# Attention's two ends in a decoder block: filler pieces placed earlier at the start, the first mixing row placed earlier at the end

## The chip, the cores and the metric

The kernel runs on one core of a Trainium2 chip. A core has a matrix engine (TensorE, PE in the profile, whose weight loads are listed apart as PEld), a vector engine (VectorE, DVE), a scalar engine (ScalarE, ACT), GpSimd (POOL), and SyncE (SP), which here only issues DMA transfers. SBUF is the on-chip memory for operands, and PSUM holds the results of matmuls in eight banks. The metric is the device time of one execution in microseconds; the time of a kernel is the median over its runs.

## The reference

One block of a decoder: 2048 tokens of width 1024. A combined projection gives queries, keys, values (8 heads of 64 channels) and 512 pooling channels `u`. Half of the mixed output is stick-breaking attention, half a pooled mean of `u`; both go through one output projection, and a SwiGLU network of width 2816 follows.

```python
h = rmsnorm(x, g_mix_pre[l]) * (1.0 + scale_m) + shift_m
q, k, v, u = jnp.split(h @ w_in[l], [SB_WIDTH, 2 * SB_WIDTH, 3 * SB_WIDTH], axis=-1)
...
# stick_breaking_attention, for each block of 128 queries
z = jnp.einsum('bhqd,bhkd->bhqk', qb, kb) * inv_sqrt
mask = s_idx < t_idx
log1m = jnp.where(mask, -jax.nn.softplus(z), 0.0)
after = lax.cumsum(log1m, axis=3, reverse=True) - log1m
w = jnp.where(mask, jnp.exp(jax.nn.log_sigmoid(z) + after), 0.0)
out = jnp.einsum('bhqk,bhkd->bhqd', w, vb)
...
mix = jnp.concatenate([attn, pool], axis=-1) @ w_out[l]
x = x + gate_m * rmsnorm(mix, g_mix_post[l])
h = rmsnorm(x, g_ffn_pre[l]) * (1.0 + scale_f) + shift_f
f = (jax.nn.silu(h @ w_gate[l]) * (h @ w_up[l])) @ w_down[l]
x = x + gate_f * rmsnorm(f, g_ffn_post[l])
```

A weight is the sigmoid of its own score times the product of the sigmoids of the negated scores between key and query. The kernel computes that product as a running product over the keys, from the last to the first.

## The kernel before

The program goes through a prologue (conditioning, the first half of the projections), attention (about 273 to 789 us), the mixing rows and the feed-forward network. Products that must be exact in float32 are made of three matmuls each: an operand is split into a rounded part and the rest (`split`, L56 to L60: a cast on ScalarE at L59, a subtract on VectorE at L60), and `mm3` (L63 to L71) adds high by high, high by low and low by high.

**Attention.** A unit is a head, a block of 512 queries and a block of 512 keys, `(h, tb, sc)`. There are 80 units, first all heads for the query blocks 0 and 1, then all heads for 2 and 3. A unit has four steps of 128 queries each, so there are 320 steps, and `n` counts them. What a step does runs through the engines:

- `weights_step` makes the scores `z` on TensorE (L926, L927), and two sigmoids on ScalarE, `sg` of the score (L929) and `pr` of the negated score (L931). It puts the block into the list `scans`.
- `scan_step` makes the running product on VectorE (L942 on a diagonal unit, L945 elsewhere; the order lists name this instruction SCALAR_TENSOR_TENSOR, the trace TENSOR_TENSOR_SCAN), with small copies of the carry on GpSimd (L941, L944, L948), and multiplies by `sg` on GpSimd into `w` (L950).
- `turn_step`, seven steps later (`OFF`), transposes four tiles of `w` on TensorE (L961) into `wt` and splits that: cast `wth` on ScalarE, subtract `wtl` on VectorE.
- `values_step`, two steps behind (`LAG`), adds the products with the values into `av` (L976, L977). The last one of a query block copies `av` to `o` (L981), and two DMAs of SyncE's queue store it to DRAM as a high and a low part, `mtd` and `mld` (L983).

PSUM banks in attention: the scores take `z0` and `z1` in turn, the transposes `w0`, `w1` and `a1`, the values `a0`, the filler pieces `mm`. Bank `z2` holds `begin`, a constant of the scans.

**Fillers.** The projections of the second half of the tokens are cut into pieces and put between the steps. A piece is three matmuls (L69 to L71) of 128x512; eight pieces make a tile of q, k or u, and the last one is followed at once by its evacuation, for q and k a cast (L59) and a subtract (L60), then a DMA store (L362). A ninth turn of each tile is empty. The loop takes as many pieces by step `n` as `goal` says: `START // 2` before attention, one more a step up to `START`, then in proportion to the attention work done.

**Loads.** `block_loads` allocates a query tile `qt` from two buffers and loads it by two DMAs (L876), keys by two more (L882) and values by one (L883). A query tile can be loaded only when the last score of the tile two back is done. Names in the lists are `qt4_1` for head 4, query block 1, and `o1_3_0` for the output of head 3, query block 0; `kd0_3` is the stored key tile of heads 0 and 1 for tokens 1536 to 2047.

**Mixing rows.** A row of 128 tokens is loaded (`mix_load`: attention's high and low part and the pooled half, L1036 and L1044), summed on GpSimd (`mix_add`, L1048), split into `mh` and `ml` in two halves of four 128-channel tiles (`mix_split`), and multiplied with the output weights in 16 pieces (`mix_products`, a bank of `f_ps` for each half of the columns). Rows 0 and 4 come first in the sequence, and `FIRST_LOADS`, `FIRST_ADDS` and `FIRST_SPLITS` say at which `n` they are loaded, added and split.

**What sets the order.** On TensorE, ScalarE, VectorE and GpSimd the instructions stand in the order in which the code writes them (`manual_schedule`, L147): the loop below is the schedule. The order of the DMAs on SyncE's queue is not written by hand; the framework's scheduler sets it when the kernel is built, and the queue issues them in that order, each waiting for its own condition. So an edit in the loop can also change the order of DMAs that the edit does not name.

## Time and profile before

| what | value |
|---|---|
| time of the runs, median of 3 | 2256.32 us (2255.94 to 2257.32) |
| the profiled execution's own time | 2255.57 us |
| its span, first to last instruction | 2253.8 us |
| TensorE busy | 2229.1 us, 99% |
| VectorE busy | 1624.3 us, 72% |
| GpSimd busy | 1267.2 us, 56% |
| ScalarE busy | 1167.7 us, 52% |
| mean granted TensorE clock | 0.999 |

Times in the profile count from the span's start. A row of the timeline gives the start, the busy time, the engine, the line, the operation, output and inputs by the program's names without their numbers, the shapes and a count; in brackets stands how long the engine sat idle before it and whose work ended that. Matmuls are pipelined: a busy time of 0.39 us belongs to one that starts 0.23 us after the one before. The shares of busy time are averages over the whole program, and attention has other ones than the feed-forward network.

### The profile page before, as it was taken

Reading aid. Unit: us, or ns where it says so; the run is one execution under the profiler, and the core shown is the slowest. Engines: PE = TensorE matmul, PEld = TensorE weight load, DVE = VectorE, ACT = ScalarE, POOL = GpSimd, SP = SyncE. Lnnn points to the kernel's source line nnn. Section 1 sums busy time; section 2 is a strip of 40 time slices with the busy share of each in tenths; the row PEclk is TensorE's granted clock in tenths of the full one; section 3 lists DMA queues with packets and bytes.
Section 4 is the critical chain, followed back from the end, with each engine's and each line's share of the span. In section 5 each row is a group of like instructions: output and inputs, shape, how many; then the busy total and the mean of one; then the engine's idle time right before and its main releaser. Section 6 shows DMA issues by size and latency. Waiting matters only on the chain.

```text
span 2253.8 us, 33256 instructions
## 1 busy us (share of the span) xinstructions
PE 2229.1 (99%) x10613; PEld 1844.2 (82%) x10613; DVE 1624.3 (72%) x2227; ACT 1167.7 (52%) x2425; POOL 1267.2 (56%) x1579
## 2 busy tenths in 40 slices
PE   8999999999999999999999999999999999999998
PEld 6888888888888888878888888888888888888887
DVE  7874599999999957666565656787866565655566
ACT  6335599898999944453232323555532323234444
POOL 1452277787779955546868687221677565651003
PEclk9999999999999999999999999999999999999999
DMA  9996877534443556665454556777853333328664
GB/s 318 341 285 214 282 196 190 147 105 119 121 118 104 175 173 219 216 198 178 157 166 154 165 163 205 262 226 244 254 168 122 94 117 94 112 91 296 216 188 149
DMA packets 323980, 413.55 MB, mean 183 GB/s; under 512 B 20630, under 2 KB 189146, under 8 KB 323676
## 3 DMA queue, kind: packets, MB, share of 16 engines
q1 hardware_dynamic: 319196, 408.81, 57.0%
q10 hardware_dynamic: 4608, 2.63, 0.4%
q8 instruction: 83, 1.36, 0.2%
q14 instruction: 93, 0.76, 0.1%
HBM read 282.90 MB, written 128.45 MB: 183 GB/s over the span
## 4 chain that ended last, share of the span: by engine, by line
PE 88%; DVE 5%; ACT 2%; issue 2%; DMA 2%; POOL 1%; SPq 0%; DVEq 0%; ACTq 0%; POOLq 0%
PE wt L961 4%; PE t_u L70 3%; PE t_u L69 3%; PE t_u L71 3%; PE t_g L69 3%; PE t_g L70 3%; PE t_g L71 3%; PE dn1p L69 3%; PE dn1p L70 3%; PE dn1p L71 3%; PE b_u L69 3%; PE dn0p L71 3%; PE b_u L70 3%; PE b_u L71 3%; PE dn0p L70 3%; PE dn0p L69 3%
## 5 line engine op out<-in xcount | busy, mean ns | idle before, releaser
L950 POOL TENSOR_TENSOR w<-sg,pr 128x512 f32<-128x512 f32 (+2 forms) x320 | 306.6, 958 | 46.8 <-DVE pr L945 16.1
L1335 POOL TENSOR_TENSOR s<-s,cu 128x512 f32<-128x512 f32 x88 | 131.8, 1504 | 237.3 <-DVE cu L1334 141.8
L945 DVE TENSOR_TENSOR_SCAN pr<-pr,carry,begin 128x512 f32<-128x512 f32 x192 | 243.8, 1270 | 0.0
L929 ACT ACTIVATE sg<-z 128x512 f32<-128x512 f32 (+2 forms) x320 | 184.1, 575 | 50.9 <-PE z L927 40.8
L60 DVE TENSOR_TENSOR wtl<-wt,wth 128x512 fp32r<-128x512 f32 (+1 forms) x320 | 189.1, 591 | 18.1 <-ACT wth L59 16.1
L59 ACT CAST wth<-wt 128x512 fp32r<-128x512 f32 (+1 forms) x320 | 183.4, 575 | 12.1 <-PE wt L961 12.1
L931 ACT ACTIVATE pr<-z 128x512 f32<-128x512 f32 (+2 forms) x320 | 183.6, 574 | 0.0
L961 PE MATMUL wt<-ident,w 128*128 128x128 f32 x1088 | 172.6, 273 | 1.9 <-POOL pr L941 1.1
L60 DVE TENSOR_TENSOR u_s_l<-u_s,u_s_h 128x512 fp32r<-128x512 f32 x66 | 64.2, 972 | 150.0 <-ACT u_s_h L59 150.0
L961 PEld LDWEIGHTS wt<-ident,w 128*128 128x128 f32 x1088 | 134.1, 140 | 33.3 <-POOL pr L941 1.8
L1325 ACT ACTIVATE s<-s 128x512 f32<-128x512 f32 x88 | 55.7, 633 | 184.1 <-DVE s L1324 184.1
L976 PE MATMUL av<-wth,vt 128*128 128x512 f32 (+1 forms) x320 | 126.4, 395 | 0.9 <-ACT o L981 0.8
L60 DVE TENSOR_TENSOR u_a_l<-u,u_a_h 128x512 fp32r<-128x512 f32 x66 | 75.6, 1147 | 64.1 <-ACT u_a_h L59 64.1
L977 PE MATMUL av<-wtl,vt 128*128 128x512 f32 (+1 forms) x320 | 118.1, 369 | 1.9 <-DVE wtl L60 1.6
L69 PE MATMUL dn0p<-w0p_h,g0p_h 128*128 128x512 f32 x308 | 119.8, 389 | 0.0
L70 PE MATMUL dn0p<-w0p_l,g0p_h 128*128 128x512 f32 x308 | 119.8, 389 | 0.0
L71 PE MATMUL dn0p<-w0p_h,g0p_l 128*128 128x512 f32 x308 | 119.8, 389 | 0.0
L926 PE MATMUL z<-kt,qt 128*128 128x512 f32 (+2 forms) x320 | 118.6, 371 | 0.7 <-ACT pr L931 0.6
L59 ACT CAST g_s_h<-g_s 128x512 fp32r<-128x512 f32 x66 | 39.5, 621 | 152.1 <-POOL g_s L1267 76.0
L927 PE MATMUL z<-kt,qt 128*128 128x512 f32 (+2 forms) x320 | 116.9, 365 | 0.0
L59 ACT CAST u_s_h<-u_s 128x512 fp32r<-128x512 f32 x66 | 38.6, 614 | 150.8 <-POOL u_s L1267 149.0
L69 PE MATMUL dn1p<-w1p_h,g1p_h 128*128 128x512 f32 x292 | 113.6, 389 | 0.0
(655 smaller groups left out, 7178.4 us busy)
## 6 DMA issues: line engine op xcount, KB each, us to landing
g<-in_w_gate_dram SPq DMA_DIRECT2D x42, 512.0 KB, 5.4
u<-in_w_up_dram SPq DMA_DIRECT2D x42, 512.0 KB, 4.1
wc<-in_w_cond_dram SPq DMA_DIRECT2D x32, 512.0 KB, 7.5
qt<-qd SPq DMA_DIRECT2D x64, 256.0 KB, 4.0
kt<-kd SPq DMA_DIRECT2D x96, 128.0 KB, 3.2
vt<-vd SPq DMA_DIRECT2D x48, 256.0 KB, 4.1
wd<-in_w_down_dram SPq DMA_DIRECT2D x44, 256.0 KB, 3.3
tdt<-wd SPq DMA_DIRECT2D x44, 256.0 KB, 2.0
```

The costliest lines, as they stand in the source:

```text
L59: nc.scalar.copy(hi, src)
L60: low.tensor_tensor(lo, src, raw(hi), ALU.subtract)
L69: nc.tensor.matmul(ps, lh, rh, start=first and i == 0, stop=False)
L70: nc.tensor.matmul(ps, lh, rl, start=False, stop=False)
L71: nc.tensor.matmul(ps, ll, rh, start=False, stop=last and i == n - 1)
L929: nc.scalar.activation(sg[:, 0:L], z[:, 0:L], AF.Sigmoid, scale=0.125)
L931: nc.scalar.activation(pr[:, 0:L], z[:, 0:L], AF.Sigmoid, scale=-0.125)
L945: nc.vector.tensor_tensor_scan(keys, keys, begin, carry, ALU.mult, ALU.bypass)
L950: nc.gpsimd.tensor_tensor(w[:, 0:L], sg[:, 0:L], pr[:, 1:L + 1], ALU.mult)
L961: nc.tensor.transpose(wt[:, i * P:(i + 1) * P], wss[u][i][:, b * P:(b + 1) * P], ident)
L976: nc.tensor.matmul(av[:, lo0:], vb, wh[:, lo0:], start=first, stop=False)
L1335: nc.gpsimd.tensor_tensor(s, s, u, ALU.mult)
```

## The change

The start: `START` goes from 6 to 8, so four pieces instead of three stand before attention and eight instead of six are taken by its fourth step. A clause runs a scan at once at `n < 4`, where the loop otherwise keeps one back.

The end: row 0 is loaded 18 steps before the end of the scores instead of 14, added 11 instead of 6, and split 6 instead of 3. `EARLY_PIECES` (four, since `HK` is 4) of its products are put one by one behind the last four steps with scores, and the bank for them is `mm`, which the fillers have left by then; the cycle of the later banks starts one place further.

```diff
-    START = 6
+    START = 8
...
-    f_ps = bank_cycle("z0", "z1", "z2", "mm", "w0", "w1", "a0", "a1")
+    f_ps = bank_cycle("mm", "z0", "z1", "z2", "w0", "w1", "a0", "a1")
...
-    FIRST_LOADS = (len(steps) - 14, len(steps) - 10)
-    FIRST_SPLITS = (len(steps) - 3, len(steps) + 2)
-    FIRST_ADDS = (len(steps) - 6, len(steps) - 1)
-    PER_STEP = 3
+    FIRST_LOADS = (len(steps) - 18, len(steps) - 10)
+    FIRST_SPLITS = (len(steps) - 6, len(steps) + 2)
+    FIRST_ADDS = (len(steps) - 11, len(steps) - 1)
+    PER_STEP, EARLY_PIECES = 3, HK
...
-        if len(scans) > 1 or n >= len(steps) and scans:
+        if len(scans) > 1 or (n < 4 or n >= len(steps)) and scans:
             scan_step(*scans.pop(0))
...
         if n >= len(steps):
             mix_pieces(PER_STEP)
+        elif n >= len(steps) - EARLY_PIECES and products:
+            mix_pieces(1)
```

Three places show what this moves. A row gives the line, the operation, the output and the inputs with the numbers of the program's names, and the shape.

ScalarE at attention's start, before: the sigmoids of the first unit's blocks, `sg0_0_0_i` and `pr0_0_0_i`, and the cast of the finished q tile `q0_2`.

```order
L931 ACTIVATE pr0_0_0_1_2677<-z0_0_0_1_2672 128x256
L929 ACTIVATE sg0_0_0_2_2689<-z0_0_0_2_2686 128x384
L931 ACTIVATE pr0_0_0_2_2691<-z0_0_0_2_2686 128x384
L929 ACTIVATE sg0_0_0_3_2706<-z0_0_0_3_2703 128x512
L931 ACTIVATE pr0_0_0_3_2708<-z0_0_0_3_2703 128x512
L59 CAST q0_2_2717<-q0_2_2649 128x512
L929 ACTIVATE sg0_1_1_0_2732<-z0_1_1_0_2729 128x128
```

The same place after:

```order
L931 ACTIVATE pr0_0_0_1_2684<-z0_0_0_1_2679 128x256
L929 ACTIVATE sg0_0_0_2_2696<-z0_0_0_2_2693 128x384
L931 ACTIVATE pr0_0_0_2_2698<-z0_0_0_2_2693 128x384
L59 CAST q0_2_2710<-q0_2_2649 128x512
L929 ACTIVATE sg0_0_0_3_2717<-z0_0_0_3_2714 128x512
L931 ACTIVATE pr0_0_0_3_2719<-z0_0_0_3_2714 128x512
L929 ACTIVATE sg0_1_1_0_2736<-z0_1_1_0_2733 128x128
```

The cast of the q tile moved from behind the fourth block's sigmoids to ahead of them. VectorE has the same order there in both kernels: scan of `pr0_0_0_2`, evacuation of `q0_2`, scan of `pr0_0_0_3`.

SyncE's queue in the middle of the first half, before: the query tile of head 4, block 1, in two halves, a key store, the output of head 3, block 0, and the next query tile.

```order
L983 DMA mtd1_97<-o1_2_1_3759 64x512
L983 DMA mld1_101<-o1_2_1_3759 64x512
L876 DMA qt4_1_3939<-qd2_1_69 64x2x512 x2
L362 DMA kd0_3_79<-k0_3_3834 128x2x512
L983 DMA mtd0_96<-o1_3_0_3869 64x512
L983 DMA mld0_100<-o1_3_0_3869 64x512
L876 DMA qt5_0_4145<-qd2_0_68 64x2x512 x2
```

The same place after (`wu0_1_32` is a chunk of projection weights):

```order
L983 DMA mtd1_97<-o1_2_1_3767 64x512
L983 DMA mld1_101<-o1_2_1_3767 64x512
L446 DMA wu0_1_32_5060<-in_w_in_dram 128x8x128
L362 DMA kd0_3_79<-k0_3_3792 128x2x512
L876 DMA qt4_1_3945<-qd2_1_69 64x2x512
L983 DMA mtd0_96<-o1_3_0_3873 64x512
L983 DMA mld0_100<-o1_3_0_3873 64x512
L876 DMA qt4_1_3945<-qd2_1_69 64x2x512
L876 DMA qt5_0_4155<-qd2_0_68 64x2x512 x2
```

A weight load and the key store moved ahead of the query tile, and its second half moved behind the two stores of head 3's output. In the same way one of a pair of key loads moved ahead of head 2's query tile.

VectorE at attention's end, before: the scans (`pr`), the subtracts behind the transposes (`wtl`), and the low part of mixing row 0 (`ml_0`).

```order
L60 TENSOR_TENSOR wtl7_3_3_3_11070<-wt7_3_3_3_11067,wth7_3_3_3_11069 128x128
L945 SCALAR_TENSOR_TENSOR pr7_3_1_2_11059<-pr7_3_1_2_11059,carry7_3_2_2_10981,begin_2659 128x512
L60 TENSOR_TENSOR wtl7_3_2_0_11102<-wt7_3_2_0_11096,wth7_3_2_0_11101 128x512
L945 SCALAR_TENSOR_TENSOR pr7_3_1_3_11088<-pr7_3_1_3_11088,carry7_3_2_3_11005,begin_2659 128x512
L60 TENSOR_TENSOR wtl7_3_2_1_11128<-wt7_3_2_1_11122,wth7_3_2_1_11127 128x512
L945 SCALAR_TENSOR_TENSOR pr7_3_0_0_11114<-pr7_3_0_0_11114,carry7_3_1_0_11043,begin_2659 128x512
L60 TENSOR_TENSOR wtl7_3_2_2_11152<-wt7_3_2_2_11146,wth7_3_2_2_11151 128x512
L60 TENSOR_TENSOR ml_0_11158<-m32_0_10858,mh_0_11157 128x512 x2
L945 SCALAR_TENSOR_TENSOR pr7_3_0_1_11140<-pr7_3_0_1_11140,carry7_3_1_1_11063,begin_2659 128x512
```

The same place after:

```order
L60 TENSOR_TENSOR wtl7_3_3_3_11071<-wt7_3_3_3_11068,wth7_3_3_3_11070 128x128
L60 TENSOR_TENSOR ml_0_11082<-m32_0_10748,mh_0_11081 128x512 x2
L945 SCALAR_TENSOR_TENSOR pr7_3_1_2_11060<-pr7_3_1_2_11060,carry7_3_2_2_10982,begin_2662 128x512
L60 TENSOR_TENSOR wtl7_3_2_0_11108<-wt7_3_2_0_11102,wth7_3_2_0_11107 128x512
L945 SCALAR_TENSOR_TENSOR pr7_3_1_3_11094<-pr7_3_1_3_11094,carry7_3_2_3_11006,begin_2662 128x512
L60 TENSOR_TENSOR wtl7_3_2_1_11134<-wt7_3_2_1_11128,wth7_3_2_1_11133 128x512
L945 SCALAR_TENSOR_TENSOR pr7_3_0_0_11120<-pr7_3_0_0_11120,carry7_3_1_0_11044,begin_2662 128x512
L60 TENSOR_TENSOR wtl7_3_2_2_11162<-wt7_3_2_2_11156,wth7_3_2_2_11161 128x512
```

The pair `ml_0` moved ahead of three scans. On TensorE the row's first four pieces stand, one each, behind the transposes `wt7_3_2_1`, `wt7_3_2_2`, `wt7_3_2_3` and `wt7_3_1_0`. From the feed-forward network on, TensorE's order is the same in both.

## The prediction

> **What bounds the kernel now.** I read the page's first part and its chain that ended last, then a table of busy time by stage, then single rows at the three places where the change moves work.
>
> ```profile
> span 2253.8 us, 33256 instructions
> PE 2229.1 (99%) x10613; PEld 1844.2 (82%) x10613; DVE 1624.3 (72%) x2227; ACT 1167.7 (52%) x2425; POOL 1267.2 (56%) x1579
> PE 88%; DVE 5%; ACT 2%; issue 2%; DMA 2%; POOL 1%; SPq 0%; DVEq 0%; ACTq 0%; POOLq 0%
> ```
>
> TensorE is busy for 2229.1 of 2253.8 us, and the change leaves every matmul in place. So only TensorE's waits can shrink or grow: 24.7 us in the whole program. The next table has, for four stretches of attention, TensorE, its weight loads, VectorE, ScalarE and GpSimd as busy us with a count, then the granted clock, DMA share and GB/s.
>
> ```profile
> 275.00:285.00 10.00, 8.67 (x44) 6.78 (x43) 7.20 (x9) 8.15 (x21) 5.63 (x17) 1.00 1.06 271
> 285.00:345.00 60.00, 59.26 (x349) 49.94 (x348) 58.71 (x84) 55.08 (x140) 45.31 (x102) 1.00 0.70 186
> 500.00:700.00 200.00, 200.00 (x1132) 168.33 (x1131) 197.55 (x248) 181.72 (x401) 161.05 (x349) 1.00 0.43 120
> 780.00:795.00 15.00, 13.99 (x72) 10.66 (x73) 14.43 (x18) 11.71 (x25) 12.98 (x24) 1.00 0.79 288
> ```
>
> At the start TensorE is idle 1.33 of 10 us, at the end 1.01 of 15; between them it is nearly full, with VectorE at 58.71 of 60 us (98%) beside it. The overlapped ends of matmuls hide some idle time in these sums, so below I measure a wait as a row's start less the end that the rows before imply at the usual spacing of 0.23 us for a 128x512 matmul. Both ends together hold about 4.3 us of waits (1.8, 1.8 and 0.7, below), which is 0.19%: the change cannot be worth more unless it mends something elsewhere. I count a difference within 0.2%, 4.5 us, as none that a measurement of this kernel can tell.
>
> **Start: two more pieces ahead of the first transpose.**
>
> ```profile
> 276.23 0.40 PE L69 MATMUL q<-hth,wq_h 128*128 128x512 f32 x1
> 276.92 0.40 PE L926 MATMUL z<-kt,qt 128*128 128x512 f32 x1
> 278.72 0.38 PE L926 MATMUL z<-kt,qt 128*128 128x256 f32 x1 [0.31 <-ACT pr L931]
> 279.55 0.45 PE L926 MATMUL z<-kt,qt 128*128 128x384 f32 x1 [0.33 <-ACT pr L931]
> 282.37 0.33 PE L961 MATMUL wt<-ident,w 128*128 128x128 f32 x1 [0.69 <-POOL pr L941]
> ```
>
> One filler piece is three matmuls: 276.92 - 276.23 = 0.69 us. The three bracketed waits, taken from the spacing, cost 0.47, 0.49 and 0.85 us: 1.8 together. Now the engines that they wait for.
>
> ```profile
> 278.55 0.59 ACT L59 CAST q<-q 128x512 fp32r<-128x512 f32 x1
> 279.17 0.69 DVE L60 TENSOR_TENSOR q<-q,q 128x512 fp32r<-128x512 f32 x1 [1.51 <-ACT q L59]
> 279.78 3.19 DVE L942 TENSOR_TENSOR_SCAN pr<-pr,zero,begin 128x512 f32<-128x512 f32 x4
> 281.22 1.09 POOL L950 TENSOR_TENSOR w<-sg,pr 128x512 f32<-128x512 f32 x1 [2.52 <-ACT pr L931]
> ```
>
> The fourth transpose waits for the multiply at 281.22, which waits for the scan at 279.78, which stands behind the evacuation of the finished q tile at 279.17. With START at 8 the q tile's last piece runs one step earlier, its cast ahead of the fourth score's sigmoids, and VectorE evacuates it while those still run. The scan then starts when its input is there, about 279.4, and the multiply ends near 281.95 instead of 282.31. TensorE does two pieces more before that transpose and reaches it near 282.1. The transposes come 0.3 us sooner and with 2 x 0.69 = 1.4 us more filler done: 1.7 saved of 1.8. Bounds: all 1.8, or the 0.3 alone if VectorE, near full afterwards, takes the rest back as waits. I take 1.7, since the table leaves VectorE 60 - 58.71 = 1.29 us of slack by 345 and TensorE can spend the lead there. The clause that runs the first four scans at once adds nothing: at that place VectorE's order is the same in both kernels, the third scan, the q evacuation, the fourth scan.
>
> **Middle: two query loads come later on SyncE's queue.** A query tile reuses the buffer of the one two back, so a load can go only when a head's last score is done. Rows in order of time: the loads' release, the stores and the next load, and the score that needs them.
>
> ```profile
> 340.75 0.40 PE L927 MATMUL z<-kt,qt 128*128 128x512 f32 x1
> 341.19 1.28 SPq L876 DMA_DIRECT2D qt<-qd  x2
> 343.85 0.67 ACT L981 COPY o<-av 128x512 f32<-128x512 f32 x1
> 344.63 0.48 SPq L983 DMA_DIRECT2D mtd<-o  x1
> 345.15 0.75 SPq L983 DMA_DIRECT2D mld<-o  x1
> 346.77 1.28 SPq L876 DMA_DIRECT2D qt<-qd  x2
> 347.95 0.22 PE L926 MATMUL z<-kt,qt 128*128 128x128 f32 x1
> qt<-qd SPq DMA_DIRECT2D x64, 256.0 KB, 4.0
> ```
>
> Before, both halves of head 4's second query tile are issued at 341.19, at once after the release (R, about 341.0), and the score that needs them runs at 347.95, R + 7.0. After, its second half stands behind the two stores of head 3's output. Those need the output copy at 343.85, so they go at R + 3.6 to R + 4.2 and end about R + 4.9; the half is issued then, and at the page's 4.0 us it lands at R + 8.9 to R + 9.4. One filler piece fewer lies between release and need, so TensorE wants it at R + 6.7 to R + 7.0: 1.9 to 2.7 us late. I take a new wait of 2.2 us. Bounds: 3.0, if the stores' 1.23 us count in full after a late copy; 0, if the copy runs as much sooner as the k tile's evacuation, which moves up, frees ScalarE and VectorE.
>
> ```profile
> 343.46 0.68 DVE L60 TENSOR_TENSOR k<-k,k 128x512 fp32r<-128x512 f32 x1
> 345.83 0.45 PE L977 MATMUL av<-wtl,vt 128*128 128x384 f32 x1 [0.35 <-DVE wtl L60]
> 305.32 1.28 SPq L876 DMA_DIRECT2D qt<-qd  x2
> 306.65 0.60 SPq L882 DMA_DIRECT2D kt<-kd  x1
> 311.68 0.22 PE L926 MATMUL z<-kt,qt 128*128 128x128 f32 x1
> ```
>
> That evacuation, 0.68 us on VectorE, now leaves this place, and the 0.35 us wait behind it goes (0 to 0.8): I take -0.4. Head 2's tile at 305.32 is overtaken by one key load, half of a pair, and needed one piece (0.69) sooner: 305.32 + 1.28 + 4.0 = 310.6 is 1.1 us early today, and the key load's 0.60 and 0.69 eat that. I take 0.3 (0 to 0.6). The other heads' loads keep their places; those of the second half of the tokens come far ahead.
>
> **End: the first mixing row's products among the last scores.** Four pieces (2.8 us) move from behind attention to one after each of four steps.
>
> ```profile
> 779.91 0.50 PE L976 MATMUL av<-wth,vt 128*128 128x512 f32 x1 [0.44 <-ACT o L981]
> 783.08 0.31 PE L976 MATMUL av<-wth,vt 128*128 128x128 f32 x1
> 784.76 0.50 PE L977 MATMUL av<-wtl,vt 128*128 128x512 f32 x1
> 786.53 0.50 PE L977 MATMUL av<-wtl,vt 128*128 128x512 f32 x1
> 788.22 0.33 PE L961 MATMUL wt<-ident,w 128*128 128x128 f32 x1 [0.41 <-POOL w L950]
> 792.17 0.50 PE L977 MATMUL av<-wtl,vt 128*128 128x512 f32 x1 [0.40 <-DVE wtl L60]
> ```
>
> By spacing the waits of the last four rows are 0.31, 0.38, 0.57 and 0.56: 1.8 us. Each is TensorE ahead of VectorE or GpSimd, and each has a piece (0.69) put ahead of it. But the row's low part must then be made sooner on VectorE.
>
> ```profile
> 782.86 1.27 DVE L945 TENSOR_TENSOR_SCAN pr<-pr,carry,begin 128x512 f32<-128x512 f32 x1
> 788.16 2.18 DVE L60 TENSOR_TENSOR ml<-m,mh 128x512 fp32r<-128x512 f32 x2
> 791.46 0.66 DVE L60 TENSOR_TENSOR wtl<-wt,wth 128x512 fp32r<-128x512 f32 x1
> 788.38 1.42 POOL L950 TENSOR_TENSOR w<-sg,pr 128x512 f32<-128x512 f32 x1
> L60 DVE TENSOR_TENSOR ml<-m,mh x32: 679/684/1784, 788.2 to 965.3; 128x512 fp32r<-128x512 f32 x32
> ```
>
> The pair of subtracts, 2.1 us at 788.16, moves ahead of the scan at 782.86, so the scans and evacuations up to the third one shift by 2.1. The first piece, at 783.1, waits with its third product for the first subtract, to about 784.0: 0.4 lost. The evacuation that ended at 784.70 ends at 786.8, and TensorE, two pieces further, stands there at 786.3: 0.45 lost. Behind that VectorE is as far as before (791.46 stays) while TensorE has four pieces more behind it, so the rest of the waits is covered. 1.8 - 0.4 - 0.45: gain 1.0. The wait at 779.91 for an output copy, 0.7 by spacing, stays, since the pieces come behind it. ScalarE's two casts, moved likewise, cost nothing beside its 11.71 busy of 15 us; if that cover went, one cast, 0.59 as at 278.55, would show. GpSimd's add moves some 10 us ahead, out of this stretch, and I count it at nothing; uncovered it is one more multiply, 1.09. Bounds: 1.8, or -0.4 if the pair is slower there. For that see the row with 679, 684 and 1784 ns: alone a subtract takes 0.68, beside GpSimd up to 1.78, and at 788.38 GpSimd's multiply took 1.42 where it usually takes 1.09. A pair blocked twice by whole multiplies takes 2 x (0.68 + 1.09) = 3.5 us, 1.4 more than at 788.16.
>
> The Trainium skill, SBUF — State Buffer, "Who interferes with whom", speaks against this change: VectorE's second port is shared with GpSimd under an exclusive lock. By that rule a subtract of two SBUF operands, put where GpSimd multiplies back to back, pays the blocked price; the trace agrees so far, with 1784 ns against 679, and the sum would be the one dearer by 1.4 us.
>
> **Sum.** -1.7 + 2.2 + 0.3 - 0.4 - 1.0 = -0.6 us. The profiled execution took 2255.57 us, 0.75 below the median of the three runs, 2256.32. From the execution I get 2255.0; from the median, which I compare with, 2255.7.
>
> **Rivals.**
> - *The query load is in time.* The output copy moves up with the evacuation gone, or the half lands in less than 4.0 us: without 2.2 and 0.3, -3.1, which is 2253.2. For it: the 4.0 is a median. Against: the copy must come over 2 us sooner.
> - *VectorE takes the start's gain back* (the other side). At 98% busy it stays the limit from 285 to 345, the two pieces' lead returns as waits, and only 0.3 of 1.7 is left: +0.8, 2257.1; with a load wait of 3.0 it is 2257.9. It turns the sign once more than 0.6 us is lost. Against: TensorE's own 0.74 us idle in that stretch.
> - *The low part is blocked by GpSimd.* The end gives -0.4 instead of 1.0: +0.8, 2257.1. For it: 12.98 busy of 15 us on GpSimd. Against: the median of the 32 subtracts is 0.68.
> - *The change doesn't do what it says*: the scan clause indeed moves no scan. If the two pieces also gain nothing and the end nothing, the loads' waits alone stand: +2.1, 2258.4.
> - *A wider slip*: a load or buffer that the order does not show as late holds every head, over 4.5 us.
>
> **How the numbers follow.** Forecast 0.42, load in time 0.2, VectorE 0.15, GpSimd's block 0.1, no gains 0.05, wider slip 0.08. The forecast's own range is 2254.6 to 2256.9. The range of eight in ten goes from the second case, 2253.2, down 0.3 for the runs' scatter, to the fifth, 2258.4. All but the slip lie within 0.2% (2251.8 to 2260.8): same 0.89, slower 0.08, and 0.03 for faster, which needs 4.5 us where the ends hold 4.3.
>
> **What would show it.** Right at the start: no wait over 0.3 us on the fourth score's neighbours, the fourth transpose with the lead of two pieces. Right in the middle: a TensorE wait of about 2 us on a query load near 350, its second half issued behind the output's stores. Right at the end: mixing products between scores from 783, one short wait for the low part, none at the third evacuation. The prediction is wrong if that load's wait is absent or over 3 us, if waits on VectorE between 285 and 345 grow by over 1 us, or if the subtract pair lasts over 3 us.

## The result: slower by 3.2 us, just above the range

The changed kernel takes 2259.24 us (median of 22 runs, 2257.60 to 2260.85), the kernel before 2256.06 (22 runs, 2254.67 to 2258.24). The ratio is 1.0014, with a 95% interval of 1.0008 to 1.002: slower by 3.2 us or 0.14%. That is within the 0.2% that I had set as the bound of "same", but it is a real loss, and it lies 0.8 us above the range. Three runs far above the others of their kernel (8001.32 and 2473.77 us in two of the experiments, 4389.62 us in the kernel before) are left out of the medians below.

The first part of the page after and the first line of its chain that ended last:

```profile
span 2257.0 us, 33253 instructions
PE 2229.8 (99%) x10613; PEld 1844.5 (82%) x10613; DVE 1624.0 (72%) x2227; ACT 1166.0 (52%) x2425; POOL 1271.6 (56%) x1579
PE 84%; DVE 7%; ACT 3%; issue 2%; POOL 2%; DMA 2%; SPq 0%; DVEq 0%; POOLq 0%; ACTq 0%
```

TensorE's busy time is the same (2229.8 against 2229.1), so its waits grew with the span: 27.2 us against 24.7. The chain leaves TensorE more often, and VectorE's share of it went from 5% to 7%. To find the place I summed, stage by stage, the distance between the starts of consecutive matmuls less the usual distance of that pair of shapes. Worked out in this way from all matmul rows of the two profiled executions, TensorE waits, in us:

| stage | before | after | difference | forecast |
|---|---|---|---|---|
| attention's first eight steps | 1.65 | 1.21 | -0.4 | -1.7 |
| from there to 324 us | 3.49 | 3.66 | +0.2 | +0.3 (head 2's load) |
| 324 to 378 us (the late query load) | 6.04 | 7.70 | +1.7 | +1.8 (2.2 - 0.4) |
| 378 to 768 us | 28.71 | 29.12 | +0.4 | 0 |
| attention's end | 5.05 | 3.42 | -1.6 | -1.0 |
| mixing rows, 795 to 987 us | 2.03 | 4.94 | +2.9 | no term |
| sum | | | +3.1 | -0.6 |

Second profiles of the two kernels give 4.41 for attention's end before and 4.43 for the mixing rows after, so a stage is known to about 0.6 us. The middle and the end came near the forecast. Two stages did not: the start gave a quarter of its gain, and 2.9 us were lost in a stage for which I had no term at all.

**The start.** Rows of the timeline after, on TensorE, ScalarE and VectorE:

```profile
279.89 0.50 PE L69 MATMUL q<-hth,wq_h 128*128 128x512 f32 x1 [1.23 <-DVE q L60]
...
278.53 0.59 ACT L59 CAST q<-q 128x512 fp32r<-128x512 f32 x1 [0.96 <-PE z L927]
...
279.50 0.60 ACT L931 ACTIVATE pr<-z 128x512 f32<-128x512 f32 x1
...
279.15 0.69 DVE L60 TENSOR_TENSOR q<-q,q 128x512 fp32r<-128x512 f32 x1 [0.54 <-ACT q L59]
280.14 1.65 DVE L942 TENSOR_TENSOR_SCAN pr<-pr,zero,begin 128x512 f32<-128x512 f32 x2 [0.30 <-ACT pr L931]
```

The eighth piece fills the first q tile, and the ninth belongs to the next tile. All pieces share the one bank `mm`, so the ninth has to wait until VectorE has evacuated the tile, 279.15 + 0.69 = 279.84; it starts at 279.89. By spacing that one wait is 1.48 us, in place of the three short ones (1.8 together). The scan that I put at 279.4 starts at 280.14: ScalarE makes the cast first and has the fourth block's sigmoid done only at 279.50 + 0.60. The cast itself comes no sooner than before (278.53 against 278.55). The tile's last matmul starts at 277.64 instead of 277.84, but by the trace what releases the cast is the score right behind that piece (L927, 278.11 + 0.39).

**The middle.** The timeline after: the queue of SyncE, and on TensorE a wait that I thought would go and the score that needs the load:

```profile
345.14 0.46 SPq L983 DMA_DIRECT2D mtd<-o  x1
345.65 0.59 SPq L983 DMA_DIRECT2D mld<-o  x1
346.29 2.75 SPq L876 DMA_DIRECT2D qt<-qd  x3
...
346.83 0.44 PE L977 MATMUL av<-wtl,vt 128*128 128x384 f32 x1 [0.58 <-DVE wtl L60]
350.29 0.30 PE L926 MATMUL z<-kt,qt 128*128 128x128 f32 x1 [1.18 <-DMA qt<-qd]
```

This is the step that the prediction described: the second half issued at 346.29 behind the two stores, and a new wait of 1.18 us (1.34 by spacing, 1.57 in a second profile; forecast 2.2, bounds 0 to 3.0). The wait for `wtl` that should have gone is still there, at 346.83.

**The end.** Rows of TensorE and VectorE in the timeline after:

```profile
781.89 0.50 PE L976 MATMUL av<-wth,vt 128*128 128x512 f32 x1 [0.44 <-ACT o L981]
...
784.84 1.32 DVE L60 TENSOR_TENSOR ml<-m,mh 128x512 fp32r<-128x512 f32 x2
...
784.95 0.65 POOL L944 COPY pr<-carry 128x1 f32<-128x1 f32 x1
785.53 0.67 POOL L948 COPY carry<-pr 128x1 f32<-128x1 f32 x1
```

The wait for an output copy stays, as said. The four waits behind it are gone, and one of 0.27 by spacing stands at 786.30. The pair of subtracts took 1.32 us, not the 2.1 of its old place nor the 3.5 of the blocked case. GpSimd, whose rows (the last two) stand beside the pair, waited instead: of the 192 copies that each of these two lines makes, with a median of 0.19 us, these two alone took 0.65 and 0.67. All eleven profiles of kernels with the pair at this place show the same. The Trainium skill's rule (SBUF — State Buffer, "Who interferes with whom") had spoken for the dearer price, with VectorE as the one that waits; the trace agrees that one of the two waits, but here it was GpSimd, and the pair kept its short time.

**The mixing rows.** The stretch of 860 to 945 us in the table of busy time (columns as in the prediction's: length, then TensorE, its weight loads, VectorE, ScalarE and GpSimd, the clock, the DMA share, GB/s), before:

```profile
860.00:945.00 85.00, 85.00 (x405) 71.02 (x404) 59.51 (x105) 40.21 (x97) 46.27 (x42) 1.00 0.65 216
```

and after:

```profile
860.00:945.00 85.00, 83.05 (x392) 68.68 (x391) 58.56 (x103) 40.20 (x96) 45.84 (x42) 1.00 0.64 214
```

TensorE in the timeline of that stretch, before:

```profile
888.56 1.03 PE L132 MATMUL f_pt<-ident,xr 128*128 128x128 f32 x8
889.35 0.48 PE L69 MATMUL mix<-wo_hbhi,mh 128*128 128x512 f32 x1
```

and after:

```profile
889.12 1.03 PE L132 MATMUL f_pt<-ident,xr 128*128 128x128 f32 x8
891.21 0.47 PE L69 MATMUL mix<-wo_hbhi,mh 128*128 128x512 f32 x1 [1.06 <-DVE x L1182]
915.85 0.47 PE L69 MATMUL mix<-wo_hbhi,mh 128*128 128x512 f32 x1 [0.84 <-DVE x L1182]
```

Before, TensorE has no idle time there and runs 405 matmuls; after, 392, and 13 x 0.23 us = 3.0 us. From the eight transposes to the next product it takes 889.35 - 888.56 = 0.79 us before and 891.21 - 889.12 = 2.09 after: a wait of 1.30 by spacing. The one at 915.85 is 1.09 in the same way. Both wait for VectorE's `x` (L1182, which was L1180 before), the norm step that reads a row's two banks of `f_ps` and frees them.

Behind the early pieces TensorE's order is the same in both kernels. But behind attention the hand-written order ends: it begins again only at the last row, and between the two the framework's scheduler sets the order of all engines when the kernel is built (what stands above on the order of the four engines holds outside this stretch). It set another one. GpSimd's queue at row 1, before (`m32_6` is the sum of row 6, `mr1_r` and `fr1_r` the two inverse roots of row 1's norms, at L123):

```order
L1048 TENSOR_TENSOR m32_2_11713<-m32_2_11713,l32_2_11715 128x512
L123 TENSOR_TENSOR fr4_r_11484<-fr4_v_11482,mhalf_185 128x1
L123 TENSOR_TENSOR mr1_r_11583<-mr1_v_11581,mhalf_185 128x1
L1182 TENSOR_TENSOR x1_1_11577<-x1_1_11577,xr1_11574 128x512 x2
L1048 TENSOR_TENSOR m32_6_11823<-m32_6_11823,l32_6_11825 128x512
L123 TENSOR_TENSOR fr1_r_11594<-fr1_v_11592,mhalf_185 128x1
```

The same place after:

```order
L1048 TENSOR_TENSOR m32_2_11713<-m32_2_11713,l32_2_11715 128x512
L123 TENSOR_TENSOR fr4_r_11484<-fr4_v_11482,mhalf_185 128x1
L123 TENSOR_TENSOR mr1_r_11583<-mr1_v_11581,mhalf_185 128x1
L1184 TENSOR_TENSOR x1_1_11577<-x1_1_11577,xr1_11574 128x512 x2
L123 TENSOR_TENSOR fr1_r_11594<-fr1_v_11592,mhalf_185 128x1
L1048 TENSOR_TENSOR m32_6_11823<-m32_6_11823,l32_6_11825 128x512
```

The sum of row 6 moved behind `fr1_r`. Two more moves belong to it: SyncE's load of row 6's low part went behind row 1's residual, two stores and the next row's high part, and on VectorE both halves of `ml_2` went back, so that the second one stands right behind `mr1_v` and not ahead of it. GpSimd at that place in the timeline, before:

```profile
836.68 0.91 POOL L123 TENSOR_TENSOR mr_r<-mr_v,mhalf 128x1 f32<-128x1 f32 x1 [3.54 <-DVE mr_v L121]
838.58 2.54 POOL L1182 TENSOR_TENSOR x<-x,xr 128x512 f32<-128x512 f32 x2 [0.99 <-DVE x L1180]
841.26 1.29 POOL L1048 TENSOR_TENSOR m<-m,l 128x512 f32<-128x512 f32 x1
842.58 0.55 POOL L123 TENSOR_TENSOR fr_r<-fr_v,mhalf 128x1 f32<-128x1 f32 x1
```

and after:

```profile
837.97 2.06 POOL L123 TENSOR_TENSOR mr_r<-mr_v,mhalf 128x1 f32<-128x1 f32 x1 [2.94 <-DVE mr_v L121]
840.95 2.54 POOL L1184 TENSOR_TENSOR x<-x,xr 128x512 f32<-128x512 f32 x2 [0.92 <-DVE x L1182]
845.00 0.55 POOL L123 TENSOR_TENSOR fr_r<-fr_v,mhalf 128x1 f32<-128x1 f32 x1 [1.51 <-DVE fr_v L121]
845.52 1.29 POOL L1048 TENSOR_TENSOR m<-m,l 128x512 f32<-128x512 f32 x1
```

Row 6's sum waits 1.51 us on GpSimd for something that it does not need, and comes 845.52 - 841.26 = 4.26 us later, while the steps around it (`x`, 838.58 to 840.95) are 2.37 later. The other price is in the first row: one element per partition, to the power of -1/2, takes 2.06 us instead of 0.91. VectorE beside it, in the timeline after:

```profile
837.74 0.68 DVE L60 TENSOR_TENSOR ml<-m,mh 128x512 fp32r<-128x512 f32 x1
838.34 0.69 DVE L60 TENSOR_TENSOR b11l<-f_h,b11h 128x512 fp32r<-128x512 f32 x1
838.94 0.69 DVE L60 TENSOR_TENSOR b21l<-f_h,b21h 128x512 fp32r<-128x512 f32 x1
840.07 1.41 DVE L1182 SCALAR_TENSOR_TENSOR x<-mix,mr_r,gm 128x512 f32<-128x512 f32 x2 [0.44 <-POOL mr_r L123]
```

Three subtracts of two SBUF operands stand back to back from 837.74 to 839.63, and the power ends at 837.97 + 2.06 = 840.03, behind the last of them; VectorE itself then waits for it. Here the Trainium skill's rule (SBUF — State Buffer, "Who interferes with whom": a VectorE instruction with two SBUF inputs contends with a GpSimd instruction that reads SBUF, and the loser is fully blocked) agrees with the trace, 2.06 us against 0.55 for the same operation at 845.00. ScalarE passes the delay on, and VectorE two rows later has the step that frees the banks; the steps between are not shown one by one, and the experiments test the link. Their timeline before:

```profile
842.59 0.62 ACT L59 CAST mh<-m 128x512 fp32r<-128x512 f32 x1 [0.28 <-POOL m L1048]
...
886.64 1.40 DVE L1180 SCALAR_TENSOR_TENSOR x<-mix,mr_r,gm 128x512 f32<-128x512 f32 x2
```

and after:

```profile
846.84 0.62 ACT L59 CAST mh<-m 128x512 fp32r<-128x512 f32 x1 [2.17 <-POOL m L1048]
...
890.31 1.41 DVE L1182 SCALAR_TENSOR_TENSOR x<-mix,mr_r,gm 128x512 f32<-128x512 f32 x2
```

On ScalarE the next row's squares stand behind that cast. At the place of the wait that step comes 890.31 - 886.64 = 3.67 us later, TensorE only 889.12 - 888.56 = 0.56. Before, the step started 888.56 - 886.64 = 1.92 ahead of TensorE's eight transposes; now it starts 1.19 behind them, and TensorE waits 1.30.

### The profile page after: what moved, and what is told of

Its sections match the earlier page's. It is cut to its first block, busy times and chain, and to the rows that moved or that the text cites. A ratio compares the mean times of both kernels' runs of the same rounds, so it can differ in the third digit from the quotient of the medians.

```text
span 2257.0 us, 33253 instructions
## 1 busy us (share of the span) xinstructions
PE 2229.8 (99%) x10613; PEld 1844.5 (82%) x10613; DVE 1624.0 (72%) x2227; ACT 1166.0 (52%) x2425; POOL 1271.6 (56%) x1579
## 4 chain that ended last, share of the span: by engine, by line
PE 84%; DVE 7%; ACT 3%; issue 2%; POOL 2%; DMA 2%; SPq 0%; DVEq 0%; POOLq 0%; ACTq 0%
PE wt L961 4%; PE t_u L71 3%; PE t_u L69 3%; PE t_u L70 3%; PE t_g L69 3%; PE t_g L70 3%; PE t_g L71 3%; PE dn1p L70 3%; PE dn1p L71 3%; PE dn1p L69 3%; PE b_u L69 3%; PE b_u L71 3%; PE b_u L70 3%; PE dn0p L70 3%; PE dn0p L71 3%; PE dn0p L69 3%
## 5 line engine op out<-in xcount | busy, mean ns | idle before, releaser
L927 PE MATMUL z<-kt,qt 128*128 128x512 f32 (+2 forms) x320 | 116.8, 365 | 0.0
L942 DVE TENSOR_TENSOR_SCAN pr<-pr,zero,begin 128x128 f32<-128x128 f32 (+3 forms) x128 | 111.4, 871 | 3.6 <-ACT pr L931 3.5
```

## The experiments

The theory: the framework's reordering of three instructions in the mixing rows costs 2.4 to 2.9 us, the query load 1.3, the bank at the start takes the gain there, and the end gains what it should. The rivals: (a) the rows pay not for their order but because four pieces (2.8 us) now stand ahead of attention's last output, so that the chain of the rows begins later; (b) the loss is in attention, in the start's part of the change, and the rows would have had it anyway.

Times below are medians of 10 or 11 runs, each against the kernel before on the same chip (21 to 33 runs). In brackets stand the ratio to the kernel before and its 95% interval; the ratio is not taken from the two medians and differs from theirs by up to 0.0003. The intervals are about 2 us to either side, so a median alone separates little; each verdict leans on a wait in the trace as well.

The profiles give a finer measure: the distance from the first filler matmul ahead of attention to the start of the last product of the mixing rows (271.29 to 982.51 in the kernel before). It is 711.2 and 710.6 us in two profiles of the kernel before, 714.2 and 714.0 in two of the whole change, 712.5 and 712.4 in two of the end alone, and 713.0 in the start alone. Two profiles of one kernel differ by 0.1 to 0.6 us in it.

**Each half of the change alone.** The end alone (`START` stays 6, no clause):

```diff
-    FIRST_LOADS = (len(steps) - 14, len(steps) - 10)
+    FIRST_LOADS = (len(steps) - 18, len(steps) - 10)
...
+        elif n >= len(steps) - EARLY_PIECES and products:
+            mix_pieces(1)
```

> Only the end's part: START stays 6, no clause on the first scans. Theory (the framework's order of the mixing rows costs the time): attention's end gains about 1.0 us, TensorE then waits about 2.9 us in all in the mixing rows, the two large waits near 890 and 915 on VectorE's multiply of a mixing row; about +1.9 us against the kernel before, 2258.0. Rival (the start's later order of loads is what delays the rows): no wait in the mixing rows, -1.0 us, 2255.1.

The start alone (`START` 8 and the clause, the end as before):

```diff
-    START = 6
+    START = 8
...
-        if len(scans) > 1 or n >= len(steps) and scans:
+        if len(scans) > 1 or (n < 4 or n >= len(steps)) and scans:
```

> Only the start's part: START 8 and the clause on the first scans; the end as before. Theory: first q tile's bank costs a wait of about 1.5 us near 280, the query load of head 4 a wait of about 1.3 us near 350, none of more than 0.3 us in the mixing rows; net of the start's gain about +1.1 us, 2257.2. Rival (the start delays the rows): the waits near 890 and 915 are there, +3 us or more, 2259.

The end alone: 2258.10, +1.95 us (1.0008, 0.9999 to 1.0017). By spacing its rows wait 5.03 us, attention's end 3.42: the same as with the whole change, with `mr1_r` at 2.07 us and the moved sum. The start alone: 2258.04, +1.89 (1.0010, 1.0001 to 1.0019), and its rows wait 2.05, as before. So the reordering comes with the end's part, and both halves lose. The two add up to 3.84, which with their intervals is the whole change's 3.2. Rival (b) is half right: attention's start does lose, but the rows' share is apart from it. In the start alone both of its waits stand in TensorE's timeline:

```profile
280.11 0.50 PE L69 MATMUL q<-hth,wq_h 128*128 128x512 f32 x1 [1.23 <-DVE q L60]
...
350.56 0.30 PE L926 MATMUL z<-kt,qt 128*128 128x128 f32 x1 [1.22 <-DMA qt<-qd]
```

**The query load.** The start alone, with a third buffer for the query tiles, so that a load need not wait for the score that ends late:

```diff
-        qt = qkp.tile([P, 2, TB], F32R, tag="qt", name=f"qt{h}_{tb}")
+        qt = qkp.tile([P, 2, TB], F32R, tag="qt", bufs=3, name=f"qt{h}_{tb}")
```

> The start's part with three buffers for query tiles instead of two, so that a query load waits no more for the head before. Theory: the 1.3 us wait near 350 is gone, the one on the first tile's bank near 280 stays; about -0.4 us against the kernel before, 1.3 us or more below the start's part alone, 2255.6. Rival (the loads were not what cost the middle): same time as the start's part alone, about 2257.2.

2257.40, +1.25 (1.0004, 0.9995 to 1.0013). The score follows without a wait, and the stage of 324 to 378 us falls from 7.73 in the start alone to 6.32 (before: 6.04). Its timeline:

```profile
350.41 0.22 PE L926 MATMUL z<-kt,qt 128*128 128x128 f32 x1
```

In the trace the load is worth 1.4 us, by the medians 0.6, with an interval that holds both. What is left of the start's loss, +1.25, is not explained by a single wait; its interval reaches below nothing. Only a part of it stands in attention and the rows: from the first filler matmul to the last product this kernel takes 711.5 us, 0.3 and 0.8 more than the two profiles of the kernel before. And the median of the spans is only 1.0 longer. In five of the eleven runs 1.97 to 2.88 us of the time lie outside the span from first to last instruction, and in five of the other kernel with a third query buffer 1.93 to 2.98; no run of any other kernel here that enters a median has over 1.9. Why is not shown.

**The bank at the start.** Four pieces ahead of attention as in the change, but only six by its first steps (`START` 6), so that the first tile isn't finished so soon; the clause is in:

```diff
-    for _ in range(START // 2):
+    for _ in range(4):
...
-    taken = START // 2
+    taken = 4
...
-        goal = min(START, START // 2 + n) + (N_PIECES - START) * spent / (4 * sum(area[:END]))
+        goal = min(START, 4 + n) + (N_PIECES - START) * spent / (4 * sum(area[:END]))
```

> START stays 6, but four pieces instead of three stand ahead of attention (with the clause on the first scans): the first q tile is finished a step sooner, no other piece moves. Theory (the second q tile's first piece, which waits for the bank of the first, ate the start's gain): no wait on the bank near 280, the three waits of the start, 1.8 us by the usual spacing, fall to about 1.0: -0.5 us, 2255.6. Rival (an evacuation that stands ahead of the fourth block's sigmoids delays the chain by as much as it saves): the waits stay near 1.8, same time as before.

2256.97, +0.48 (1.0002, 0.9993 to 1.0011). The wait for the bank is gone, and another of the same size stands in its place in the timeline:

```profile
280.35 0.39 PE L926 MATMUL z<-kt,qt 128*128 128x256 f32 x1 [1.50 <-ACT pr L931]
```

The stage waits 1.72 against 1.65 before. So even without the bank a piece put ahead of attention bought nothing here: the scores then meet ScalarE's sigmoids in one long wait. The bank is what one sees, but not the limit.

This run also shows how far the mixing rows scatter. Their order is that of the kernel before, and nothing in attention's end is changed, yet they wait 2.9 us by spacing. Two of GpSimd's sums waited 1.91 and 0.92 us for their loads, and one TensorE wait of 0.86 stands at 914.51. So a wait below about 0.9 us in one profile's rows doesn't tell one kernel from another.

**Fewer early pieces at the end.** `EARLY_PIECES` 3 and then 2, the rest of the end's part as in the change:

```diff
-    PER_STEP, EARLY_PIECES = 3, HK
+    PER_STEP, EARLY_PIECES = 3, 3
```

> The end's part with three early pieces instead of four (START 6, no clause). Of the mixing rows' order only this differs: GpSimd's sum of row 6 stands ahead of the small power operation of row 1 again, as in the kernel before. Theory (the order is the cause): no TensorE wait over 0.3 us in the mixing rows, attention's end gains 0.7 to 1.0 us: -0.8 us, 2255.2. Rival (attention's last output comes later by the pieces put ahead of it, and the rows' chain with it, in whatever order): three quarters of the delay stay, TensorE waits 1 to 2 us near 890 and 915, +0.5 to +1.2 us, 2256.9.

> The end's part with two early pieces (1.4 us of work ahead of attention's end, inside the margin), the mixing rows in the order of the kernel before. Theory: no wait over 0.5 us in the rows, the end gains 0.5 to 0.9 us: 2255.4. Rival: as three early pieces or worse, 2256.0 or more.

With either the framework keeps the order of before in the rows. Three: 2256.01, -0.14 (1.0, 0.9992 to 1.0009), rows 2.47, attention's end 4.09. Two: 2255.88, -0.23 (1.0, 0.9991 to 1.0009), rows 2.06, end 4.63. One early piece fewer, and the whole loss of the end's part is gone; but so is a part of its gain.

**Two pieces a step behind the scores.** The end alone with `PER_STEP` 2:

> The end's part with four early pieces, and two instead of three behind each later step; the order of the mixing rows then is that of the kernel before but for two rows. Theory: no wait over 0.5 us in the mixing rows, gain at the end 1 to 1.6 us: 2255.0. Rival (late end of attention): waits of 1 us or more near 890 and 915, about 2257 or more.

2256.82, +0.3 (1.0003, 0.9994 to 1.0012), and TensorE waits 0.94, 0.98 and 0.87 by spacing at three places of the rows. I had expected no waits. The framework had moved yet another load, that of row 2, and more instructions around it: GpSimd stood idle for 3.9 us together ahead of its sums of rows 2 and 6, until their loads had landed. This run tells the theory and the rivals apart no better than the first.

**Row 6's sum put back.** The end alone, with the code of row 6's load and sum placed ahead of row 1's normalisation, and a dependence that forces the order: `fr1_r` takes its exponent from a cell that two small GpSimd operations make out of the sum (it is still -1/2). This adds those two operations, 0.19 us each, and nothing else to the work.

```diff
+            cell = added[SEQUENCE[n + 3]][1][:, 0, 0:1]
+            e = op.tile([P, 1], F32, tag="after", bufs=1, name="after_sum")
+            nc.gpsimd.tensor_tensor(e, cell, cell, ALU.subtract)
+            nc.gpsimd.tensor_tensor(e, e, mhalf, ALU.add)
+            exponent[f"fr{T}"] = e
```

> The end's part with all four early pieces, and GpSimd's sum of row 6 put ahead of row 1's power operation again by a false dependence (two GpSimd instructions of 128x1 more, some 0.3 us); every other engine's order and the load order as in the end's part alone. Theory (that one order is the cause): the waits near 890 and 915 go from 1.7 and 1.1 us to 0.5 us or less together, the end's gain of 1.6 us stays: 2255.2, about 3 us below the end's part alone. Rival (the rows' chain is late because attention ends later and because the load and VectorE's order differ): the waits stay within 0.5 us, 2258.

2256.58, level with the kernel before on that chip (1.0, 0.9991 to 1.0009), where the end alone had lost 1.95 on another. To set it beside the end alone and the whole change on one chip, I ran all of them again, with the kernel before once more for a second profile of its rows:

> The kernel before once more, for a second profile: how far do single executions differ in the mixing rows? Theory: no TensorE wait over 0.5 us between 860 and 940, and the sum of row 12 on GpSimd waits 0.2 to 0.9 us for its load, as the landing happens to fall. Rival (the waits in the rows come and go with the execution): a wait of 0.8 us or more near 890 or 915 here too.

> The whole change again, on one chip with the two below: +3.2 us against the kernel before (2.5 to 3.9), TensorE waiting 2.0 to 3.3 us in the mixing rows. Rival (the mixing waits differ from chip to chip): under 1.5 us of waits there.

> The end's part alone again: +1.9 us against the kernel before, waits of 2.3 to 3.3 us in the rows. Rival (chip to chip): the same time as the next kernel.

> The end's part with row 6's sum put ahead again, on the same chip as the end's part alone. Theory (that order costs 1.3 us in the rows' chain): 1.3 to 2 us below the end's part alone, GpSimd's sum of row 6 some 1.9 us sooner than there. Rival: within 0.5 us of it.

The kernel before waits 2.05 us in the rows in this profile too. Whole change 2258.96, +3.16 (1.0013, 1.0004 to 1.0022); end alone 2257.83, +2.03 (1.0007, 0.9999 to 1.0016); end alone with the dependence 2256.58, +0.78 (1.0004, 0.9996 to 1.0013). The dependence takes 1.25 us off. GpSimd's sum of row 6 in the timeline of the end alone:

```profile
845.18 1.29 POOL L1048 TENSOR_TENSOR m<-m,l 128x512 f32<-128x512 f32 x1
```

and with the dependence:

```profile
837.52 2.06 POOL L125 TENSOR_TENSOR mr_r<-mr_v,mhalf 128x1 f32<-128x1 f32 x1 [2.94 <-DVE mr_v L123]
...
843.24 1.29 POOL L1050 TENSOR_TENSOR m<-m,l 128x512 f32<-128x512 f32 x1 [0.21 <-DMA l<-mld]
```

The sum comes 1.94 us sooner. But VectorE keeps its own new order, `mr1_r` still takes 2.06 us, and two waits remain in the rows (0.62 and 1.13 by spacing, against 1.10 and 1.22 in the end alone). By the medians of one chip the move of the sum is worth somewhat over half of the loss. All the rows' waits together fall by 0.9 us between these two profiles and by 1.3 between the earlier two of the same kernels, and from the first filler matmul to the last product the kernel with the dependence takes 711.4 and 711.3 us.

**The whole change with both repairs** (dependence and third query buffer):

> The whole change with two mends: the false dependence that puts row 6's sum ahead again, and three buffers for query tiles. Theory: start +0.4 us (bank wait kept), no query wait near 350, end -1.6 us, mixing rows +0.5 us: about -0.6 us against the kernel before, 2255.5, and 3 to 4 us below the whole change. Rival (the loss is spread over attention and not in these two places): 2258 or more.

2256.85 (10 runs), +0.36 (1.0, 0.9991 to 1.0009), where a gain of 0.6 was expected: waits of 0.87 and 1.09 by spacing stay in the rows, from the part of the reordering that the dependence doesn't mend. Most of the 3.2 us is gone, but no gain is left.

**A late output without the change.** For rival (a): the kernel before, with extra copies of `av` to scratch on ScalarE ahead of attention's last output copy. They add work that nothing uses, and change nothing else in attention.

```diff
+            for _ in range(5 if end else 0):
+                nc.scalar.copy(up.tile([P, TB], F32, tag="um", bufs=2, name="late"), av)
```

Three, five and seven copies:

> The kernel before with three more copies of attention's last output on ScalarE ahead of the real one (128x512 each, some 0.5 us): the mixing rows' chain starts about 1.5 us later, and no other order changes. Theory (TensorE leads the rows' chain by a margin of about 2.1 us near 890, worked out from the waits and chain times of the runs so far; a later start within the margin costs nothing): waits under 0.6 us in the rows, 0 to +0.5 us, 2256.2. Rival (every delay of the chain is paid in full): +1.5 us, 2257.4.

> The same with five more copies, about 2.6 us, again in the order of the kernel before. Theory (the margin of 2.1 us is exceeded): a TensorE wait of about 0.5 us near 890 and one of about 1 us near 915, +1.3 to +2.2 us, 2257.6. Rival (what costs the time are the early pieces or the order alone, not the late end of attention): no wait over 0.5 us, within 0.4 us of the kernel before.

> The kernel before with seven more copies of attention's last output, about 3.6 us: the start of the rows' chain is 1.0 us later than with five, and the framework now gives the mixing rows the order of the end's part (row 6's load, its sum and row 2's low part later); attention is untouched. Theory after five copies cost almost nothing (the order is what carries the delay into TensorE, a late start alone is absorbed): waits of 2 us or more near 890 and 915 together, +1.5 to +3 us, 2258.3. Rival (the order does no harm without the early pieces): at most the 1.0 us of later start, +1 us, 2257.1.

Three copies (1.57 us): 2257.01, +0.90 (1.0001, 0.9993 to 1.001), one wait of 0.64 by spacing. Five (2.54 us): 2256.52, +0.41 (1.0004, 0.9995 to 1.0012), no wait over 0.31. Its timeline on GpSimd, VectorE and TensorE:

```profile
838.45 0.91 POOL L123 TENSOR_TENSOR mr_r<-mr_v,mhalf 128x1 f32<-128x1 f32 x1 [3.54 <-DVE mr_v L121]
843.51 1.29 POOL L1050 TENSOR_TENSOR m<-m,l 128x512 f32<-128x512 f32 x1 [0.64 <-DMA m<-mtd]
...
888.61 1.40 DVE L1182 SCALAR_TENSOR_TENSOR x<-mix,mr_r,gm 128x512 f32<-128x512 f32 x2
...
889.08 1.03 PE L132 MATMUL f_pt<-ident,xr 128*128 128x128 f32 x8
889.87 0.48 PE L69 MATMUL mix<-wo_hbhi,mh 128*128 128x512 f32 x1
```

and its row in the table of busy time, with 403 matmuls where the changed kernel has 392:

```profile
860.00:945.00 85.00, 84.93 (x403) 70.54 (x402) 59.52 (x105) 40.94 (x100) 45.78 (x41) 1.00 0.63 215
```

Here the last output is copied at 818.49, in the changed kernel at 818.65, before at 815.57: the same lateness, in the old order. The step that frees the banks stands at 888.61, 1.97 us later than before but still 0.47 ahead of the transposes, and TensorE does not wait there; with the change's order it stands at 890.31. So a late start alone is nearly absorbed, and between these two profiles the order adds 890.31 - 888.61 = 1.70 us. I had expected waits in this run, and that part of rival (a) falls.

Seven copies were meant to show where the lateness alone shows. Instead the framework answered them with the order of the end's part, this time with attention's order untouched (one cast on ScalarE and one step on VectorE in the rows are moved besides):

```profile
839.24 2.07 POOL L123 TENSOR_TENSOR mr_r<-mr_v,mhalf 128x1 f32<-128x1 f32 x1 [2.62 <-DVE mr_v L121]
...
846.78 1.29 POOL L1050 TENSOR_TENSOR m<-m,l 128x512 f32<-128x512 f32 x1
...
891.49 1.40 DVE L1182 SCALAR_TENSOR_TENSOR x<-mix,mr_r,gm 128x512 f32<-128x512 f32 x2
...
890.38 1.03 PE L132 MATMUL f_pt<-ident,xr 128*128 128x128 f32 x8
892.38 0.47 PE L69 MATMUL mix<-wo_hbhi,mh 128*128 128x512 f32 x1 [0.97 <-DVE x L1182]
```

2259.63 (10 runs), +3.2 (1.0014, 1.0005 to 1.0023). The step is 891.49 - 890.38 = 1.11 behind the transposes, and the wait 892.38 - 890.38 - 0.79 = 1.21, as in the changed kernel (1.19 and 1.30). From five copies to seven the output is 1.67 us later (820.16 against 818.49) but the loss goes from 0.4 to 3.2 us, each against the kernel before on its own chip, and the rows' waits go from 2.67 to 4.34. The blocked power (2.07) and the late sum come back with the order. In this kernel lateness and order act together, so its 3.2 us is not the price of the order alone.

**The early pieces without the reordering.** The end alone, but with two pieces instead of three behind the first step without scores:

```diff
-            mix_pieces(PER_STEP)
+            mix_pieces(PER_STEP - (n == len(steps)))
```

> The end's part with four early pieces, and two instead of three behind the first step after the last scores: the mixing rows stand in the order of the kernel before. Theory: TensorE's waits at the end go as in the change (1.0 to 1.6 us gained), in the rows at most 0.5 us is lost: 2255.2. Rival (the early pieces cost in the rows whatever the order): waits of 1.5 us or more there, 2256.5 or more.

The framework then keeps the order of before in the rows. 2255.78, -0.65 against before (0.9996, 0.9987 to 1.0005). Its timeline on GpSimd and TensorE:

```profile
837.47 0.91 POOL L123 TENSOR_TENSOR mr_r<-mr_v,mhalf 128x1 f32<-128x1 f32 x1 [3.54 <-DVE mr_v L121]
...
913.47 0.47 PE L69 MATMUL mix<-wo_hbhi,mh 128*128 128x512 f32 x1 [0.39 <-DVE x L1182]
```

Attention's end waits 3.40, as with the whole change (3.42), and the rows 2.81 instead of 5.03: all four early pieces are there, and most of the loss is not. The rows still wait 0.8 more than before, with one wait of 0.63 by spacing. One piece fewer stands ahead of attention's last output here, so the lateness is a little smaller too: the output copy is 70.9 us ahead of the transposes near 889, where it is 70.5 in the whole change and 73.0 before. It has the lowest median of all changed kernels, but its interval holds no change.

One reading runs through all the profiles: where VectorE's step that frees the banks near 889 stands against TensorE's transposes. With the new order it is 1.0 to 1.6 us behind them in all five (whole change and end alone twice each, seven copies). With the old order it is 0.4 to 2.4 us ahead in all ten, five of them with two to four early pieces or with three or five copies. With the dependence it is 0.5 to 0.8 behind in all three.

## Why the prediction was wrong, point by point

- **Start, -1.7 (bounds 0.3 to 1.8): wrong.** Measured -0.4, near the low bound. The step that failed is "the q tile's last piece runs one step earlier ... VectorE evacuates it while those still run". It is earlier in steps and hardly in time: the piece ends 0.2 us sooner, but the cast is released only with the score behind it and starts at 278.53 where it was at 278.55. The fourth block's sigmoids then come behind that cast and behind a score that starts at 277.87 instead of 276.92, and the scan comes at 280.14 instead of 279.4. And the piece behind the tile needs the tile's bank, a wait that I didn't look for. The run without the bank's wait shows that the gain wasn't there to be had in this form.
- **Middle, +2.2 for the query load (0 to 3.0): right, sized too high.** The mechanism is the one described, and the wait measured 1.34 by spacing; the third buffer removes it. Counted from the release R (here 341.43 + 0.23 = 341.66), the half was issued at R + 4.6 instead of R + 4.9 and landed 4.0 later, as taken; TensorE came to the score at R + 7.3 instead of R + 6.7 to R + 7.0. The -0.4 for the k evacuation did not come: the wait for `wtl` was 0.35 before and is 0.58 after. The 0.3 for head 2, whose score stands in the stage ahead, did not come either: at 312.63 it has no wait. The stage gives +1.7 where its terms made 1.8, since one term was too large and the other did not come.
- **End, -1.0 (-1.8 to +0.4): right.** -1.0 to -1.6 by the two profiles of before. The two losses in it, 0.4 at the first piece and 0.45 at the third evacuation, came to one wait of 0.27. The subtract pair was even cheaper than I took it (1.32, not 2.1): GpSimd waited for it and not it for GpSimd, so the price of a blocked pair, and its rival, fall.
- **The mixing rows, no term: this step failed and decides the sign.** I wrote that the pieces come off "from behind attention" and compared TensorE's order alone behind it, which is the same. On the queues of GpSimd and SyncE the framework had moved one instruction each, on VectorE a pair. Measured +2.4 to +2.9, where my sum had nothing. All stages as measured make +3.1 us (the table above), where my terms made -0.6. None of the three signs that I had named for being wrong came: the load's wait was there and under 3 us, the waits on VectorE from 285 to 345 did not grow, and the pair took 1.32 us. All three looked where the edit works, and none at the rows.
- **The rivals.** "VectorE takes the start's gain back" (2257.1) had the right size for the start, but not the cause: the wait lies within the first steps, on ScalarE's cast and the bank, and from there to 324 us nothing grows by more than 0.2. "The load in time" and "the low part blocked by GpSimd" are refuted by the rows at 350.29 and 784.84. "The change doesn't do what it says" gave 2258.4 by waits of the loads alone; the time was near it for another reason. The wider slip, "that the order does not show as late", came nearest in kind: the order did show it, in a stretch that I didn't read.

What stays open: the split of the rows' loss between the late sum, the slower power and the late output (the dependence takes off 1.25 us by the medians of one chip, 1.9 between two and 0.9 to 1.3 in the rows' waits); what takes time outside the span in the kernels with a third query buffer; and why the framework chose the other order (its costs are not in the trace). An experiment that puts back the order of VectorE alone was not made.

## What to carry to other kernels

An edit in a part whose order is written by hand can change the order of a later part that a scheduler lays out: compare every engine's queue up to the next place where the order is fixed, not only the queue of the engine that bounds the kernel. If a few instructions there have changed places, ask whose chain they stand in and how far the bounding engine is ahead of that chain; here it was 1.9 us (1.6 to 2.4 in four profiles with the rows untouched, and 0.4 in one where a load landed late), and a delay of 2.0 us (with TensorE itself 0.5 late) cost nothing while one of 3.7 cost 1.3 at the first place alone. Filler put ahead of a wait helps only if its own resources (here the one bank of all pieces) and the engine behind the wait are free by then.

## What the runs showed that I had not expected

- A GpSimd operation on one element per partition takes 0.55 us alone, 0.91 beside two VectorE subtracts of 128x512 and 2.06 beside three of them back to back. That is more than it looks worth, since a row's whole norm waits for it.
- A cut of one filler piece (four early pieces to three, or three to two behind the first step without scores) made the framework keep the old order of the rows, a difference of some 2 us; so did five copies against seven in a kernel where nothing else was changed.
- Landings of the same loads differ between executions of one kernel: the sum of row 6 in the kernel before stood without a wait in one profile and waited 1.07 us for its load in another, at the same time of the whole (2255.57 and 2255.12 us).
